# Two attention stages issued in text order, laid out by clocks that the generator keeps

## The chip, the core and the metric

One core of a Trainium2 chip runs the whole program as one launch. The metric is the device time of that launch in microseconds (us). Differences of more than about 0.2% can be told from the runs.

## What is computed

The input is x, 512 tokens by 1024, in float32. It goes through two blocks.

The first block has two layers. Each is a feed-forward part, a mixer and a second feed-forward part, with a conditioning vector that scales, shifts and gates each part. The mixer of the first layer is the stick-breaking attention ("stick" from here), that of the second a linear recurrence. The second block has two "hybrid" layers: three kinds of attention beside each other (A: blocks, B: the 128 best keys by an index score, C: dilated groups), whose outputs are gated, projected and added. The stick mixer and the common part of A, B and C are:

```python
z = q[block] @ k.T                       # q already scaled, 16 heads, 4 query blocks of 128
log_keep = where(s < t, log_sigmoid(-z), 0)
later = reverse_cumsum(log_keep) - log_keep
w = where(s < t, exp(log_sigmoid(z) + later), 0);  o = w @ v
...
p = softmax(where(ok, q @ k.T * hd ** -0.5, -inf));  o = p @ v
merged = sum over branches of sigmoid(m_g[branch]) * (y[branch] @ w_br[branch])
x = x + merged @ w_out
```

## The kernel before

All weights come as one stream of 128x1024 chunks in the order of their use. Each 512 columns are split in two float32r parts, `wh` (ScalarE, ACT here) and `wl` (GpSimd, POOL here, or VectorE, DVE here), and every product is three matmuls of 512 columns: high by high, high by low, low by high. TensorE (PE here) has 13646 matmuls. PSUM has eight banks: four `mm` for the projections, two `z` for scores, one `T` for transposes and one `o` for attention outputs.

A Python generator writes the program. Its projections are plain loops (`proj`, `proj_tok`), which after each three matmuls call `pump`. Everything else is a coroutine: it issues some instructions and then yields a number of us after which its next step is due. The due times count in `vt`, a clock that only the matmuls advance. So between the matmuls of a projection stand the steps of attention that are due by then.

A "pack" is one unit of attention that fills a bank with scores: for heads with a causal mask the query blocks 0 and 2, or 3, or 1 and 1 of two heads; for C two or four blocks. In stick (`unit`, lines 1108 to 1150) a pack is: scores in a `z` bank; two sigmoids on ACT (`keep`, `beta`); on POOL an affine_select for each diagonal block, on DVE a scan for each of the one or two segments (`R`, line 1133) and a product for each (line 1137); four transposes to the `T` bank; a copy on ACT and a difference on DVE for the two parts of the result (`wide`, lines 1026 and 1029). When a head has its four blocks, eight matmuls make its output in the `o` bank (`causal_pv`), and an ACT copy and a DVE sum (`osum`, line 1005) join its parts. In the hybrid layers (`softmax`, lines 1387 to 1422) a pack is, for each segment, the scores and behind them at once the masked maximum on DVE (line 1399), then the exponential with its sum on ACT (line 1411), a reciprocal and a scaling (line 1417), the transposes and the same evacuation.

Between `begin` (whose block is issued as written) and the end of stick, and in both hybrid layers, the order on the engines is not the text's: a scheduler behind the generator puts instructions of all engines in the order that its own estimates give.

Stick ends with the output product in two parts (`STICK_PARTS`): `wo0` for head pairs 0 to 5, `wo1` for pairs 6 and 7, each for eight row blocks m, added to x; after the second, `whole(m)` makes the squares (`sq`) and the parts of the next input (`gH`, `gL`). A hybrid layer ends with the branch products (`br`, each after its gate `mg`) in the order of `HYBRID_ORDER`; at the first of branch 1, `reload` reads x back, and in the first hybrid layer multiplies its eight tiles by two factors on DVE (line 1794). Then come the products of `w_out`, which read `hH` and `hL` (lines 1820 and 1823).

## Time and profile before

| | us |
|---|---|
| median of three runs | 3132.39 (3127.72 to 3134.24) |
| the profiled execution | 3133.14 |
| its span, first to last instruction | 3131.3 |
| PE busy | 3007.2 (96%) |
| DVE, ACT, POOL busy | 1921.7, 1321.7, 1072.8 |
| granted PE clock, mean | 0.986 |

Between the span and the execution's time lie 1.8 us. The stages stand in this order in the span: two feed-forward parts around stick (415 to 700), two around the recurrence, then the hybrid layers (1985 to 2545 and 2545 to 3113) and the last norm. A matmul's busy time overlaps that of the next, so that a busy PE need not be at its peak.

### The profile page before, as it was taken

The numbers are of one execution on the slowest core, as the hardware profiler recorded it, in microseconds if no ns is written. First come the engines' busy times: TensorE is split into PE (matmuls) and PEld (weight loads), VectorE is DVE, ScalarE is ACT, GpSimd is POOL, SyncE is SP. The second block draws the span as 40 slices with busy tenths as digits, with TensorE's granted clock in tenths as the row PEclk, the third lists the DMA queues.
The fourth block names the chain that finished last, engine by engine and source line by source line (L and its number), as shares of the span: only waits on it lengthen the run. The fifth ranks groups of instructions, "written<-read, shape, count | busy, mean of one in ns | idle before, by whom it ended". The sixth has DMA issues, their size and how long they took to land. (4 is left out here: it accounts for less than half of the span.)

```text
span 3131.3 us, 39192 instructions
## 1 busy us (share of the span) xinstructions
PE 3007.2 (96%) x13752; PEld 2474.4 (79%) x13752; DVE 1921.7 (61%) x3455; ACT 1321.7 (42%) x2520; POOL 1072.8 (34%) x828
## 2 busy tenths in 40 slices
PE   7999999989999999999899999999999999999998
PEld 5788877778888888887788888888787778878776
DVE  7844467685445654569773334587766547877643
ACT  3332245543332333226543333355455434655552
POOL 4455744440001100025430002433334674333356
PEclk9999999999999999999999999999999999999999
DMA  6454545324343344542222223543441336324322
GB/s 243 163 195 172 209 120 142 102 68 147 130 140 128 135 162 149 181 175 74 88 88 101 94 105 111 136 135 105 120 132 62 108 124 177 103 88 128 102 78 91
DMA packets 132358, 400.03 MB, mean 128 GB/s; under 512 B 18496, under 2 KB 19008, under 8 KB 132160
## 3 DMA queue, kind: packets, MB, share of 16 engines
q1 hardware_dynamic: 132160, 397.51, 39.1%
q8 instruction: 109, 1.79, 0.2%
q14 instruction: 89, 0.73, 0.1%
HBM read 342.91 MB, written 6.30 MB: 112 GB/s over the span
## 5 line engine op out<-in xcount | busy, mean ns | idle before, releaser
L503 POOL TENSOR_TENSOR wl<-raw,wh 128x512 fp32r<-128x512 f32 x576 | 803.0, 1402 | 940.9 <-ACT wh L497 897.2
L497 ACT CAST wh<-raw 128x512 fp32r<-128x512 f32 x968 | 596.4, 620 | 1152.7 <-PE mm L417 993.0
L417 PE MATMUL mm<-hH,wh 128*128 128x512 f32 x1584 | 620.9, 392 | 12.4 <-ACT ge L1284 9.8
L417 PE MATMUL mm<-hL,wh 128*128 128x512 f32 x1584 | 620.3, 392 | 4.1 <-DVE hL L722 3.4
L417 PE MATMUL mm<-hH,wl 128*128 128x512 f32 x1584 | 619.4, 391 | 0.3 <-POOL wl L503 0.3
L503 DVE TENSOR_TENSOR wl<-raw,wh 128x512 fp32r<-128x512 f32 x394 | 290.0, 737 | 363.0 <-ACT wh L497 360.6
L417 PE MATMUL mm<-gH,wh 128*128 128x512 f32 x1016 | 409.7, 403 | 1.9 <-ACT wh L497 1.8
L417 PE MATMUL mm<-gH,wl 128*128 128x512 f32 x1016 | 401.9, 396 | 1.3 <-POOL wl L503 1.3
L417 PE MATMUL mm<-gL,wh 128*128 128x512 f32 x1016 | 401.6, 395 | 0.0
L417 PEld LDWEIGHTS mm<-hH,wh 128*128 128x128 f32 x1584 | 299.1, 189 | 76.0 <-ACT ge L1284 10.2
L417 PEld LDWEIGHTS mm<-hL,wh 128*128 128x128 f32 x1584 | 299.0, 189 | 68.5 <-DVE hL L722 5.5
L417 PEld LDWEIGHTS mm<-hH,wl 128*128 128x128 f32 x1584 | 298.9, 189 | 62.3 <-POOL wl L503 0.7
L485 DVE CUSTOM_DVE_ANT_0 raw<-raw,cact 128x1024 f32<-128x1024 f32 x144 | 209.2, 1456 | 177.4 <-DMA raw<-ws 167.0
L417 PE MATMUL mm<-aH,wh 128*128 128x512 f32 x704 | 273.9, 389 | 0.0
L417 PE MATMUL mm<-aH,wl 128*128 128x512 f32 x704 | 273.9, 389 | 0.0
L635 POOL TENSOR_TENSOR sq<-x 128x512 f32<-128x512 f32 x7 | 8.1, 1151 | 736.9 <-DVE x L970 710.0
L417 PEld LDWEIGHTS mm<-gH,wl 128*128 128x128 f32 x1016 | 192.4, 189 | 42.1 <-POOL wl L503 2.6
L417 PEld LDWEIGHTS mm<-gH,wh 128*128 128x128 f32 x1016 | 193.4, 190 | 36.2 <-ACT wh L497 2.3
L417 PEld LDWEIGHTS mm<-gL,wh 128*128 128x128 f32 x1016 | 193.3, 190 | 32.9
L1029 DVE TENSOR_TENSOR wide<-T,wide 128x128 fp32r<-128x128 f32 (+3 forms) x192 | 94.2, 511 | 102.5 <-ACT wide L1026 93.8
L417 PEld LDWEIGHTS mm<-aH,wh 128*128 128x128 f32 x704 | 132.1, 188 | 27.6
L417 PEld LDWEIGHTS mm<-aH,wl 128*128 128x128 f32 x704 | 132.1, 188 | 27.4
(302 smaller groups left out, 4825.0 us busy)
## 6 DMA issues: line engine op xcount, KB each, us to landing
raw<-ws SPq DMA_DIRECT2D x629, 512.0 KB, 3.3
ks<-rH SPq DMA_DIRECT2D x80, 128.0 KB, 3.1
kl<-rL SPq DMA_DIRECT2D x80, 128.0 KB, 2.4
qs<-rH SPq DMA_DIRECT2D x56, 128.0 KB, 3.9
qs<-rL SPq DMA_DIRECT2D x56, 128.0 KB, 3.9
keep<-ws SPq DMA_DIRECT2D x16, 256.0 KB, 5.7
ks<-qkH SPq DMA_DIRECT2D x32, 128.0 KB, 2.8
kl<-qkL SPq DMA_DIRECT2D x32, 128.0 KB, 2.4
```

The costliest lines, as they stand in the source:

```text
L417: self.nc.tensor.matmul(out, lhsT, rhs, start=start, stop=stop, skip_group_check=True)
L485: nc.vector.tensor_tensor_reduce(raw, raw, self.cact, 1.0, 0.0, OP.mult, OP.add, accum_out=self.mods[vec][:, m:m + 1])
L497: nc.scalar.copy(h, w)
L503: eng.tensor_tensor(l, w, h.bitcast(F32), OP.subtract)
L635: nc.gpsimd.tensor_tensor(q, self.x[m], self.x[m], OP.mult)
L1029: nc.vector.tensor_tensor(dst(pt[1], o, n, step), src(c, n, step), dst(pt[0], o, n, step).bitcast(F32), OP.subtract)
```

## The change

Stick and both hybrid layers are built inside `planned`, which makes the order on PE, DVE, ACT and POOL that of the text; SP, which issues the DMAs, keeps the scheduler. To write a good text order, the generator now keeps a clock for DVE, ACT and POOL as well: `Front` and `Timed` wrap the engines, and `clocked` gives each instruction a start (when its engine is free and its operands are made), a length by formula, and an end. A matmul moves `vt` to when its operands are made. A bare `yield` means: when the instructions that this step issued have ended. `rel` gives a bank back at that time, and `room` starts a pack only while at most two heads are in work.

In `softmax` all scores of a pack come first and then the maxima. In stick the two segments of a pack are scanned and multiplied in one instruction each, over 512 columns, with one of three masks, and one affine_select does both diagonals: of 64 scans, products and affine_selects 40 are left. The parts `oH` and `oL` of stick's output are made as each pair of heads ends, and its output product is cut in pairs 0 to 3 and 4 to 7. In the hybrid layers five gates of branch 1 move ahead of the products of branch 2, and the factors of the norm are made by a coroutine beside the first projection. PE has the same 13646 matmuls.

```diff
-HYBRID_ORDER += _each(2, "mg") + _each(2, "br") + _each(1, "mg") + _each(1, "br") + [f"out{m}" for m in (0, *range(2, KD))]
+HYBRID_ORDER += (_each(2, "mg") + _each(1, "mg")[:5] + _each(2, "br") + _each(1, "mg")[5:] + _each(1, "br")) + [f"out{m}" for m in (0, *range(2, KD))]
...
-STICK_PARTS = range(0, 6), range(6, 8)
+STICK_PARTS = range(0, 4), range(4, 8)
...
-        "k_stick": np.concatenate([zero, stick], 1),
+
+        "k_stick": np.concatenate([stick, zero[:, :256], stick, zero, stick, zero[:, :128], stick, zero[:, :128], stick], 1),
...
+    @contextlib.contextmanager
+    def planned(self):
+
+        E = mybir.EngineType
+        self.timed = True
+        for e in self.clock:
+            self.clock[e] = max(self.clock[e], self.vt)
+        with self.tc.manual_schedule(engines={E.PE, E.DVE, E.Activation, E.Pool}):
+            yield
+        self.timed = False
+
...
+    def clocked(self, engine, op, args, kw):
+        aps = [x for x in (*args, *kw.values()) if hasattr(x, "tensor")]
+        out, ins = aps[0], aps[1:]
+        if "accum_out" in kw:
+            ins = [x for x in ins if x is not kw["accum_out"]]
+        n = 1
+        for q in max((x.shape[1:] for x in aps), key=lambda d: [int(np.prod(d))]):
+            n *= q
+        bank = any(x.space == bass.MemoryType.PSUM for x in ins)
...
+        start = max([self.clock[engine]] + [self.made.get(x.tensor.name, 0.0) + 0.035 for x in aps])
+        if engine == "vector":
+            d = 0.15 + n / 960.0
+            if op == "reciprocal":
+                d = 0.15 + n * 0.0062
+            elif op == "tensor_tensor_scan":
+                d = 0.15 + n / 480.0
+            elif op in ("stream_shuffle", "match_replace", "tensor_tensor_reduce"):
+                d += 0.07
+            if strided:
+                d += n * 0.0008
+            if not bank and n > 8 and op not in ("max", "match_replace"):
+                for a, b in self.pool_runs:
+                    d += 0.58 * max(0.0, min(b, start + d) - max(a, start))
...
+        end = start + d
+        self.clock[engine] = end - over
+        self.made[out.tensor.name] = end
+        if "accum_out" in kw:
+            self.made[kw["accum_out"].tensor.name] = end
...
+    def matmul_at(self, out, ins, cost, fresh):
+        t = max([self.vt] + [self.made.get(x.tensor.name, 0.0) + 0.054 for x in ins])
+        if fresh:
+            t = max(t, self.read.get(out.tensor.name, 0.0) + 0.054)
+        self.vt = (t if self.timed else self.vt) + cost
+        self.made[out.tensor.name] = self.vt + 0.17
...
+        if d is None:
+
+            d = max(0.05, self.last - self.vt + 0.05)
...
+        if not self.timed or self.op_end <= self.vt:
+            self.live[tag] -= n
+            return
+
+        def later():
+            yield self.op_end - self.vt
+            self.live[tag] -= n
+        self.spawn(later())
...
+    def room(self, heads):
+
+        me = object()
+        self.line.append(me)
+        while self.line[0] is not me or len(self.apart | set(heads)) > 2:
+            yield 0.2
+        self.line.pop(0)
+        self.apart |= set(heads)
 
...
         def unit(pk):
+            yield from self.room([head for head, _ in pk])
...
-            yield 1.5
+            yield
             R = self.t("R")
-            for head, b, c, w in segs:
-                dg = beta[:, c + w - 128:c + w]
+            mask = masks[{0: 0, 3: 1, 1: 2}[pk[0][1]]]
+
+            d = [c + w - 128 for _, _, c, w in segs]
+            dg = beta[:, d[0]:d[0] + 128]
+            if len(d) == 1:
                 nc.gpsimd.affine_select(dg, dg, [[-1, 128]], OP.is_gt, 0.0, base=0, channel_multiplier=1)
-                nc.vector.tensor_tensor_scan(R[:, c:c + w][:, ::-1], keep[:, c:c + w][:, ::-1],
-                                             mask[:, 512 - w:512][:, ::-1], 1.0, op0=OP.mult, op1=OP.max)
-            yield 2.1
-            for head, b, c, w in segs:
-                nc.vector.tensor_tensor(beta[:, c:c + w - 1], beta[:, c:c + w - 1], R[:, c + 1:c + w], OP.mult)
-            yield 1.5
+            else:
+                dg = bass.AP(tensor=dg.tensor, offset=dg.offset, ap=[list(dg.ap[0]), [d[1] - d[0], 2], [1, 128]])
+                nc.gpsimd.affine_select(dg, dg, [[0, 2], [-1, 128]], OP.is_gt, 0.0, base=0, channel_multiplier=1)
+            nc.vector.tensor_tensor_scan(R[:, ::-1], keep[:, ::-1], mask[:, ::-1], 1.0, op0=OP.mult, op1=OP.max)
+            yield
+            nc.vector.tensor_tensor(beta[:, 0:511], beta[:, 0:511], R[:, 1:512], OP.mult)
+            yield
             T = yield from self.get("T")
             for i in range(4):
                 self.transpose(T[:, 128 * i:128 * i + 128], beta[:, 128 * i:128 * i + 128])
             yield from self.causal_evac(T, pk)
-            yield 1.0
+            yield
             for head, b, c, w in segs:
                 self.left[head] -= 1
                 if self.left[head] == 0:
...
+                h = self.t("oH", dt=F32R)
+                nc.scalar.copy(h, out)
+                yield
+                l = self.t("oL", dt=F32R)
+                nc.vector.tensor_tensor(l, out, h.bitcast(F32), OP.subtract)
+                yield
...
+        yield from self.room([head for head, _, _ in pk])
...
-            at = (mx[:, i:i + 1], sm[:, i:i + 1]) if store is None else store(head, b)
-            segs.append((c, w, at))
+            segs.append((c, w, (mx[:, i:i + 1], sm[:, i:i + 1]) if store is None else store(head, b)))
+            c += w
+        for (head, b, _), (c, w, at) in zip(pk, segs):
             nc.vector.tensor_tensor_reduce(T[:, c:c + w], z[:, c:c + w], mask(head, b, w), 1.0, -3.0e38, OP.add, OP.max,
                                            accum_out=at[0])
...
-                    self.stick()
+                    with self.planned():
...
-            self.hybrid(l)
+            with self.planned():
...
```

PE in the first hybrid layer, where the fourth pack of four C blocks is scored; `z` is the bank, `ks`, `kl` and `qs` the keys and queries, `mm` a projection. Before:

```order
L417 MATMUL z_18833<-ks_18647,qs_18641 128x128
L417 MATMUL z_18833<-kl_18653,qs_18641 128x128
L417 MATMUL mm_18777<-gH_15365,wh_18684 128x512
L417 MATMUL mm_18777<-gL_15366,wh_18684 128x512
L417 MATMUL mm_18777<-gH_15365,wl_18685 128x512
L417 MATMUL z_18833<-ks_18647,qs_18641 128x128
L417 MATMUL z_18833<-kl_18653,qs_18641 128x128
L417 MATMUL mm_18778<-gH_15365,wh_18684 128x512
L417 MATMUL mm_18778<-gL_15366,wh_18684 128x512
L417 MATMUL mm_18778<-gH_15365,wl_18685 128x512
```

And now:

```order
L547 MATMUL z_18784<-ks_18640,qs_18634 128x128
L547 MATMUL z_18784<-kl_18646,qs_18634 128x128
L547 MATMUL z_18784<-ks_18640,qs_18634 128x128
L547 MATMUL z_18784<-kl_18646,qs_18634 128x128
L547 MATMUL z_18784<-ks_18640,qs_18634 128x128
L547 MATMUL z_18784<-kl_18646,qs_18634 128x128
L547 MATMUL z_18784<-ks_18640,qs_18634 128x128
L547 MATMUL z_18784<-kl_18646,qs_18634 128x128
L547 MATMUL mm_18677<-gH_15620,wh_18665 128x512
L547 MATMUL mm_18677<-gL_15621,wh_18665 128x512
```

The eight scores of the pack, which stood in pairs with projections between, now stand together, and the projections follow.

DVE at the end of stick; `R` is the scan, `beta` the product, `wide` the part of the transposed weights, `osum` the sum of a head, `oL` the part for the output product, `x` the sum with the output product, `wshift` work for the next stage. Before:

```order
L1029 TENSOR_TENSOR wide_5570<-T_5606,wide_5569 128x128
L1029 TENSOR_TENSOR wide_5570<-T_5606,wide_5569 128x3x128
L1202 SCALAR_TENSOR_TENSOR x_178<-mm_5616,mod_1767,x_178 128x512
L1029 TENSOR_TENSOR wide_5570<-T_5649,wide_5569 128x4x128
L1005 TENSOR_TENSOR osum_5602<-jt_5688,o_5676 64x512
L429 TENSOR_TENSOR oL_5697<-osum_5369,oH_5695 128x512
L1202 SCALAR_TENSOR_TENSOR x_252<-mm_5656,mod_1767,x_252 128x512
L503 TENSOR_TENSOR wl_5700<-raw_5431,wh_5699 128x512
L536 TENSOR_SCALAR wshift_5703<-raw_5431,mod_2475 128x512
L538 SCALAR_TENSOR_TENSOR wshift_5703<-raw_5431,mod_2475,wshift_5703 128x512
L429 TENSOR_TENSOR oL_5711<-osum_5602,oH_5709 128x512
```

And now:

```order
L328 TENSOR_TENSOR wide_5429<-T_5509,wide_5428 128x2x128
L328 TENSOR_TENSOR wide_5515<-T_5509,wide_5514 128x2x128
L328 TENSOR_TENSOR beta_5507<-beta_5507,R_5518 128x511
L328 SCALAR_TENSOR_TENSOR R_5551<-keep_5530,stick_3133 128x512
L328 TENSOR_TENSOR beta_5532<-beta_5532,R_5551 128x511
L328 TENSOR_TENSOR wide_5515<-T_5544,wide_5514 128x128
L328 TENSOR_TENSOR wide_5515<-T_5544,wide_5514 128x3x128
L328 TENSOR_TENSOR osum_5543<-jt_5554,o_5534 64x512
L328 TENSOR_TENSOR wide_5515<-T_5560,wide_5514 128x4x128
L328 TENSOR_TENSOR osum_5543<-jt_5576,o_5567 64x512
L328 TENSOR_TENSOR oL_5581<-osum_5543,oH_5579 128x512
L328 SCALAR_TENSOR_TENSOR x_92<-mm_5485,mod_1767,x_92 128x512
```

The sums of x with the first part of the output product (the last is `x_252`), which stood between the last packs, are now over before them, and the last pack's steps stand by themselves.

DVE in the first hybrid layer, where x is read back; `sig<-mm,inv` is a gate, `sig<-sig,mm` frees the bank of a branch product. Before:

```order
L1800 TENSOR_TENSOR sig_20785<-mm_20745,inv_15868 128x512
L1800 TENSOR_TENSOR sig_20823<-mm_20787,inv_15868 128x512
L1810 SCALAR_TENSOR_TENSOR sig_20451<-sig_20451,mm_20849 128x512
L1794 SCALAR_TENSOR_TENSOR x_20825<-x_20825,vecs,inv_15882 128x512
L1794 SCALAR_TENSOR_TENSOR x_20827<-x_20827,vecs,inv_15882 128x512
L1810 SCALAR_TENSOR_TENSOR sig_20507<-sig_20507,mm_20867 128x512
L1794 SCALAR_TENSOR_TENSOR x_20829<-x_20829,vecs,inv_15882 128x512
L1794 SCALAR_TENSOR_TENSOR x_20831<-x_20831,vecs,inv_15882 128x512
L1794 SCALAR_TENSOR_TENSOR x_20833<-x_20833,vecs,inv_15882 128x512
L1794 SCALAR_TENSOR_TENSOR x_20835<-x_20835,vecs,inv_15882 128x512
L1794 SCALAR_TENSOR_TENSOR x_20837<-x_20837,vecs,inv_15882 128x512
L1810 SCALAR_TENSOR_TENSOR sig_20583<-sig_20583,mm_20883 128x512
```

And now:

```order
L328 TENSOR_TENSOR sig_20684<-mm_20631,inv_15785 128x512
L328 TENSOR_TENSOR sig_20722<-mm_20686,inv_15785 128x512
L328 TENSOR_TENSOR sig_20760<-mm_20724,inv_15785 128x512
L328 SCALAR_TENSOR_TENSOR x_20762<-x_20762,vecs,inv_15803 128x512
L328 SCALAR_TENSOR_TENSOR x_20764<-x_20764,vecs,inv_15803 128x512
L328 SCALAR_TENSOR_TENSOR x_20766<-x_20766,vecs,inv_15803 128x512
L328 SCALAR_TENSOR_TENSOR x_20768<-x_20768,vecs,inv_15803 128x512
L328 SCALAR_TENSOR_TENSOR x_20770<-x_20770,vecs,inv_15803 128x512
L328 SCALAR_TENSOR_TENSOR x_20772<-x_20772,vecs,inv_15803 128x512
L328 SCALAR_TENSOR_TENSOR x_20774<-x_20774,vecs,inv_15803 128x512
L328 SCALAR_TENSOR_TENSOR x_20776<-x_20776,vecs,inv_15803 128x512
L328 SCALAR_TENSOR_TENSOR sig_20242<-sig_20242,mm_20786 128x512
```

The eight scalings of x, which stood between the first branch products, now all stand ahead of them.

## Rows read from the trace of the kernel before

**Rows 1.** Busy time of each engine by stage; columns as in the first row.

```profile
core 0: us, PE busy (x) PEld busy (x) DVE busy (x) ACT busy (x) POOL busy (x), PEclk, DMA share, GB/s
...
415.00:672.00 257.00, 239.87 (x1156) 195.90 (x1155) 182.27 (x288) 140.17 (x280) 115.24 (x125) 0.97 0.40 111
672.00:700.00 28.00, 21.46 (x96) 17.92 (x95) 24.80 (x41) 10.65 (x19) 12.35 (x9) 0.88 0.23 76
...
1985.00:2545.00 560.00, 536.44 (x2583) 441.04 (x2582) 384.10 (x884) 283.02 (x616) 255.54 (x195) 0.99 0.39 113
2545.00:3113.00 568.00, 551.11 (x2644) 453.94 (x2644) 365.92 (x852) 279.86 (x613) 264.34 (x207) 0.99 0.36 110
...
```

**Rows 2.** PE in order of time, two dense matmuls: start, duration.

```profile
1000.18 0.39 PE L417 MATMUL mm<-wide,wh 128*128 128x512 f32 x1
1000.41 0.39 PE L417 MATMUL mm<-aH,wl 128*128 128x512 f32 x1
...
```

**Rows 3.** As rows 1, seven stretches at half clock: the third, the sum.

```profile
682.90:689.70 6.80, 5.12 (x16) 4.47 (x17) 5.72 (x17) 0.62 (x1) 1.28 (x1) 0.50 0.24 77
...
sum 37.60, PE 33.84 PEld 27.72 DVE 28.51 ACT 13.68 POOL 9.48; mean PE 4.83 PEld 3.96 DVE 4.07 ACT 1.95 POOL 1.35
```

**Rows 4.** Waits of PE from 415 to 700: total us, times, longest.

```profile
PE o L417 <- DVE sq L639: 6.5, 1, 6.5
...
PE mm L417 <- DVE oL L429: 0.3, 1, 0.3
```

**Rows 5.** Waits of PE in the first hybrid layer, 1985 to 2545.

```profile
PE z L417 <- DVE mx L1399: 5.0, 5, 2.3
PE T L421 <- ACT T L1417: 3.5, 8, 0.9
...
PE mm L417 <- ACT hH L1820: 1.7, 1, 1.7
...
PE mm L417 <- DVE sig L1810: 1.6, 2, 1.0
...
PE T L421 <- ACT T L1411: 0.5, 1, 0.5
```

**Rows 6.** Waits of PE in the second hybrid layer, 2545 to 3113.

```profile
PE T L421 <- ACT T L1417: 3.5, 8, 1.0
...
PE mm L417 <- DVE hL L1823: 0.2, 1, 0.2
```

**Rows 7.** Groups of stick, 440 to 672: busy us, mean ns | idle before.

```profile
L1124 ACT ACTIVATE keep<-z 128x512 f32<-128x512 f32 x40 | 24.3, 606 | 10.1 <-PE z L417 9.4
...
L1133 DVE TENSOR_TENSOR_SCAN R<-keep,stick 128x512 f32<-128x512 f32 x16 | 20.2, 1263 | 4.4 <-ACT keep L1124 4.4
...
L1137 DVE TENSOR_TENSOR beta<-beta,R 128x511 f32<-128x511 f32 x16 | 13.2, 822 | 0.9
...
L1029 DVE TENSOR_TENSOR wide<-T,wide 128x512 fp32r<-128x512 f32 x16 | 10.9, 683 | 8.3 <-ACT wide L1026 8.2
...
L429 DVE TENSOR_TENSOR oL<-osum,oH 128x512 fp32r<-128x512 f32 x8 | 6.8, 858 | 3.2 <-ACT oH L427 3.1
```

**Rows 8.** Groups of the hybrid layer on ACT and DVE, 1985 to 2545.

```profile
L1411 ACT ACTIVATE T<-T,nm 128x128 f32<-128x128 f32 x48 | 19.2, 400 | 29.9 <-DVE nm L1408 15.0 <-DVE nm L1405 14.4
L1411 ACT ACTIVATION_READ_ACCUMULATOR T<-T,nm 128x1 f32 x96 | 18.0, 187 | 0.0
...
L1399 DVE CUSTOM_DVE_ANT_0 T<-z,hc 128x128 f32<-128x128 f32 x48 | 13.6, 284 | 15.3 <-PE z L417 15.2
```

**Rows 9.** DVE in order of time, where x comes back.

```profile
2482.68 0.69 DVE L1800 TENSOR_TENSOR sig<-mm,inv 128x512 f32<-128x512 f32 x1 [4.68 <-PE mm L417]
...
2485.32 2.45 DVE L1794 SCALAR_TENSOR_TENSOR x<-x,vecs,inv 128x512 f32<-128x512 f32 x2
...
2488.30 6.95 DVE L1794 SCALAR_TENSOR_TENSOR x<-x,vecs,inv 128x512 f32<-128x512 f32 x5
```

**Rows 10.** Waits of DVE in the first hybrid layer, as rows 4.

```profile
DVE wide L1029 <- ACT wide L1026: 42.9, 25, 3.8
```

More of the change, by code (lines that the diff above doesn't have):

```diff
@@ L338, in __init__ @@
         self.lines = {t: [] for t in self.BANKS}
+        self.line, self.apart = [], set()
+    @contextlib.contextmanager
[6 more added lines that the diff above has]
+            yield
+        self.timed = False
+    def clocked(self, engine, op, args, kw):
[7 more added lines that the diff above has]
+        bank = any(x.space == bass.MemoryType.PSUM for x in ins)
+        wide = [x for x in ins if int(np.prod(x.shape[1:])) > 8]
+        strided = any(abs(x.ap[-1][0]) > 1 for x in (out, *wide) if len(x.ap) > 1)
+        start = max([self.clock[engine]] + [self.made.get(x.tensor.name, 0.0) + 0.035 for x in aps])
[12 more added lines that the diff above has]
+                    d += 0.58 * max(0.0, min(b, start + d) - max(a, start))
+            over = 0.082
+        elif engine == "scalar":
+            d = (0.162 if bank else 0.2) + n / 1210.0
+            if isinstance(kw.get("bias"), type(out)) or isinstance(kw.get("scale"), type(out)):
+                d += 0.09
+            if "accum_out" in kw:
+                d += 0.187
+            if strided:
+                d += n * 0.001
+            over = 0.1
+        else:
+            two = len([x for x in ins if int(np.prod(x.shape[1:])) > 8]) > 1
+            d = 0.12 + n / (440.0 if two else 900.0)
+            over = 0.045
+            self.pool_runs = [q for q in self.pool_runs if q[1] > start - 8.0] + [(start, start + d)]
+        end = start + d
+        self.clock[engine] = end - over
+        self.made[out.tensor.name] = end
+        if "accum_out" in kw:
+            self.made[kw["accum_out"].tensor.name] = end
+        for x in ins:
+            self.read[x.tensor.name] = end
+        self.op_end = end
+        self.last = max(self.last, end)
@@ L350, in step @@
     def step(self, g):
+        before, self.last = self.last, 0.0
         try:
@@ L594, in proj_tok @@
             for b in range(4):
-                out, first = banks[b]
+                if kt == 0:
+                    outs.append(banks(b))
+                out, first = outs[b]
                 out = out[:, :used]
@@ L601, in proj_tok, with banks, get @@
                 self.pump()
+    def banks(self, tags, out):
+        def get(b):
+            out.append(self.bank(tags[b]))
+            return out[b], True
+        return get
     def mod_end(self, vec, m, n):
@@ L663, in spread @@
             self.nc.vector.tensor_scalar(d[:, 128 * b:128 * b + 128], self.ident, y[:, b:b + 1], None, OP.mult)
-        ps = self.bank(tag)
-        return d, ps
+        return d
+    def spread(self, y, tag):
+        d = self.diagonal(y)
+        return d, self.bank(tag)
     def spread_mm(self, d, ps):
@@ L1054, in causal_pv @@
                 self.mm(ps[:, 128 * kt:512], v(kt), pt[part][:, 512 * kt:512 * kt + 512 - 128 * kt], kt == 0 and part == 0, True)
+        self.apart.discard(head)
         return ps
@@ L1059, in stick @@
         nc = self.nc
-        mask = self.t("stick")
-        nc.sync.dma_start(mask, self.io["k_stick"])
+        masks = [self.t("stick") for _ in range(3)]
+        for i, t in enumerate(masks):
+            nc.sync.dma_start(t, self.io["k_stick"][:, 512 * i:512 * i + 512])
         V = {}
@@ L1178, in stick @@
             if name[0] == "v":
-                banks = [self.bank("mm") for _ in range(4)]
-                self.proj_tok(name, stat, [(b, True) for b in banks])
+                banks = []
+                self.proj_tok(name, stat, self.banks(["mm"] * 4, banks))
                 self.spawn(v_evac(n, banks))
@@ L1452, in factors @@
         def factors():
+            late = max(self.made.get(q.tensor.name, 0.0) for q in self.sq.values())
+            yield max(0.1, late - self.vt + 0.1)
             st, ys = self.stats(tag="o")
@@ L1462, in factors @@
             self.rel("o")
+            inv["row"] = row
             if self.twice:
-                d, bc = self.spread(ys[0], "o")
-                self.spread_mm(d, bc)
+                bc = yield from self.get("o")
+                self.spread_mm(ds[1], bc)
                 inv["x"] = self.t("inv")
@@ L1479, in idx_evac @@
         def idx_evac(ps):
+            while "row" not in inv:
+                yield 0.2
             kh, kl = yield from self.rope(ps[0])
@@ L1491, in v_evac @@
         def v_evac(ps, tags, heads, key):
+            while "token" not in inv:
+                yield 0.2
             for b in range(4):
@@ L1769, in driver, with attention @@
                     yield 0.5
+        self.spawn(factors(), 1.0)
         ps = self.proj("idx", self.hmov)
-        factors()
         self.spawn(idx_evac(ps))
         tags = ["mm", "z", "z", "T"]
-        banks = [self.bank(t) for t in tags]
-        self.proj_tok("vab", stat, [(b, True) for b in banks])
+        banks = []
+        self.proj_tok("vab", stat, self.banks(tags, banks))
         self.spawn(v_evac(banks, tags, 7, "AB"))
-        self.need(lambda: len(iw) == 4 and "ready" in iq)
-        self.spawn(choose())
-        self.spawn(driver())
+        def attention():
+            while len(iw) < 4 or "ready" not in iq:
+                yield 0.3
+            self.spawn(choose())
+            self.spawn(driver())
+        self.spawn(attention())
         sig = {}
```

171 lines of the change are left out of this document (103 added, 68 removed).

## The prediction

> **What bounds the kernel now.** I read the busy times by stage first [rows 1]. In the four stretches that the change rebuilds PE is busy 239.87 of 257, 21.46 of 28, 536.44 of 560 and 551.11 of 568 us: idle for 17.13, 6.54, 23.56 and 16.89, together 64.1. DVE comes next with 384.1 of 560, ACT and POOL are half idle, the DMA share is 0.4 or less. So PE bounds every one of these stages, and its work is the same 13646 matmuls afterwards: the change can only take away time in which PE stands or runs slowly. How much that is, three views tell.
>
> First the idle time, 64.1.
>
> Second, what the busy time hides. Two dense matmuls start 0.23 us apart and each is shown for 0.39 [rows 2]: a busy PE counts each matmul 0.16 longer than it costs. The tail of the last one ahead of every wait is therefore lost time shown as busy. The lists of waits have 9 lines with 21 waits in and behind stick [rows 4], 13 lines with 30 in the first hybrid layer [rows 5], 12 with 28 in the second [rows 6] (first and last line shown of each): 79 x 0.16 = 12.6.
>
> Third, the clock. In seven stretches of these stages the granted clock is 0.50, the lower of its two levels; PE is busy for 33.84 us in them [rows 3], work that takes half as long at the higher level: 16.9.
>
> Sum of what there is to gain: 64.1 + 12.6 + 16.9 = 93.6 us. The lists also say who keeps PE waiting: the chains of the attention packs (a `z` bank is not free until its maxima are taken, transposes wait for the weights), and at three places no pack but a hand-over: `o <- sq` 6.5 behind stick [rows 4], `mm <- sig` 1.6 and `mm <- hH` 1.7 at the end of a hybrid layer [rows 5].
>
> **The change part by part.**
>
> *The packs' order.* A pack that is scored at once needs other matmuls beside it until its weights are ready. In a hybrid layer a pack of four C blocks takes 4 x (0.284 + 0.082) for maxima and the small step behind each (0.082: my estimate, of the size of a 128x1 instruction, between 0.05 and 0.19 by [rows 8]), then 4 x (0.400 + 0.187) on ACT: 1.46 + 2.35 = 3.8, some 4.4 with two small steps and the hops. In the order, counted in matmuls of 512 columns at 0.227, PE has between the scores and the transposes of such a pack now 0 to 2.7 us of other matmuls before and 5.4 to 5.6 after. For packs of two segments it is 1.6 to 5.8 before (median about 3.4), 3.4 to 11.9 after (median 5.6). In stick a pack takes 0.606 + 1.263 + 0.822 = 2.69 [rows 7], after the scores, with less than before on DVE since one scan stands for two; all packs but the last few have more than 3.4 beside them. So nearly all waits on packs go. I do not take all: the durations in the generator's clocks are formulas, and an engine that is late by one instruction passes it on. My choice is that one eighth of these waits stays; from both sides it could be none, or half, which is a rival below.
>
> *The end of stick.* The last packs have too little left beside them. From scores to transposes 2.69 against about 1.3 us of matmuls in the order: 1.4 waits. From transposes to output, copy and difference, 0.606 + 0.683 = 1.29, nothing beside. From output to output product an ACT copy, `osum`, `oH`, `oL`: 0.606 + 0.68 + 0.606 + 0.858 = 2.75 (the copies priced as `keep`, `osum` as `wide`) [rows 7], nothing beside, since the first part, that covered it so far, is now issued ahead, as the second pair of order listings shows. Together 5.4. PE stands three times within a few us, so I expect one more stretch at the lower clock, of mean size: 4.83 / 2 = 2.4 [rows 3]. Bounds: 0 (if the four pairs of the second part cover it) and 10. I take 7.8, a new cost.
>
> *Behind stick.* `wo1` has now four pairs, 12 matmuls for each m, 2.72 us instead of 1.36. DVE has per m a sum, squares and a difference, three instructions between 0.683 and 0.858 [rows 7], 2.2: it lagged before, which is the 6.5 on `sq`, and keeps pace now. Left is the last m, 2.0. The half-clock stretch that stood there (5.12 busy, 2.6 lost [rows 3]) goes with the wait.
>
> *The return of x.* The eight scalings now all stand ahead of the evacuations of branch 1 on DVE. x lands, by the start of the first, 2485.32 - 2482.68 = 2.64 us after the gate ahead of it; seven of the eight take 2.45 + 6.95 [rows 9], 1.34 each, all eight 10.7; the first evacuation behind them 0.69. PE meanwhile fills its four `mm` banks, 9 matmuls each, 36 x 0.227 = 8.2. So PE waits 2.64 + 10.7 + 0.69 - 8.2 = 5.8, where it waited 1.6 before on `sig` [rows 5]. Bounds: 0, if the load of x, issued from SP, comes early, and 14, if no bank is free when it starts. The next wait, 1.7 on `hH` [rows 5], stays. In the second layer the scalings are absent, and I leave 1.0 for its end.
>
> *Edits at nothing.* The 24 scans, products and affine_selects fewer relieve DVE and POOL, which are busy 182.27 and 115.24 of 257 [rows 1]: hidden behind PE. The two mask loads more on SP stand in the begin of the program; if that cover failed, each would cost about the landing time of x, 2.64. The five gates moved ahead of branch 2 cost PE the same matmuls and DVE the same 0.69 each [rows 9]; they only lengthen the time that five `sig` tiles live. The eager `oH`, `oL` are the same instructions at another place. The factors beside the first projection: few instructions off PE, covered by it.
>
> *The sum.* Left behind: 7.8 + 2.0 + 5.8 + 1.7 + 1.0 = 18.3. Of the 93.6 the places named above made up 6.5 + 2.6 + 1.6 + 1.7 = 12.4; of the other 81.2 one eighth stays, 10.2. 93.6 - 18.3 - 10.2 = 65.1. The profiled execution took 3133.1, so 3068.0 by its own time; the median is 0.7 lower, and I predict 3067, 2.1% faster.
>
> *A rule of the skill that speaks against it.* In [rows 10] DVE has stood 42.9 us, in 25 waits of up to 3.8, at `wide`, whose other half ACT had not yet made; whatever stood behind it waited too, though a scheduler had chosen that order. The Trainium skill, page "TensorE: Matmul & The Clock Gate", section "Architectural detail: the array is 16× 32×32, not 1× 128×128", says that ScalarE and VectorE take their instructions strictly first in, first out, and that TensorE only pulls weight loads ahead. The row agrees with it. By this rule an order fixed by formula turns each late instruction into a delay of all packs behind it; the fourth rival below is what that would make of the time here.
>
> **Rivals.**
> 1. Nearly everything goes: the end of stick is covered by the second part's first pairs, and x comes early. Then 93.6 is gained: 3133.1 - 93.6 - 0.7 = 3039. For it: DVE is free for a third of the time [rows 1]. Against: the chain at the end of stick has nothing beside it in the order.
> 2. Half of the waits come back at other places, because DVE is late by more than the clocks think: of 81.2 half stays, 40.6 instead of 10.2: 3067 + 30 = 3097, and up to 3127 if nearly all do. I put its middle at 3110.
> 3. The change does not do what it says, since the matmuls that are moved between the waits leave others uncovered: within 0.2%, 6.3 us (what a measurement of this kernel can just tell from no change), 3132.
> 4. Slower, by one mechanism: DVE, in the fixed order, stands at a `wide` or a maximum whose operand is late, while a ready instruction of the other head waits behind it; the pack's bank comes free late and PE stands, once per pack. There are 40 packs in stick and 46 in each hybrid layer, 132. All the gain is eaten at 93.6 / 132 = 0.71 us per pack, more than that is slower. The 42.9 / 25 = 1.7 us of a mean wait [rows 10] show that such delays are of that size; at 1 us per pack the loss is 132 and the time 3132 + 132 - 94 = 3170. Against it: PE is not held up by most of those 42.9 us today, and after the change a pack has 2 us more cover.
>
> **How the numbers follow.** My forecast, with its own range 3050 to 3095: 0.62. Rival 1, 3039: 0.12. Rival 2, 3110: 0.16. Rival 3: 0.03. Rival 4: 0.07. The range for 8 in 10 takes in the forecast, most of rival 1 and the near half of rival 2, by the bounds on the end of stick, the return of x and the share that stays: 3038 to 3116. Faster by over 0.2%: 0.62 + 0.12 + nearly all of 0.16, less the part of rival 2 that ends above 3126: 0.88. Within: 0.04. Slower: 0.08.
>
> **What would show it.** Right: PE idle in the hybrid layers falls from 23.6 and 16.9 to under 12 and 6, the lines `z <- mx` and `T <- T` of the waits all but vanish, of seven half-clock stretches at most three are left. A new wait of PE of 4 to 7 us on the evacuation behind the scalings of x, and three waits of 1 to 3 us at the end of stick, on DVE and ACT; no wait of 6.5 on `sq`. Wrong: PE waits spread over all packs, with DVE waiting on ACT's `wide` for more than 42.9 us (rival 4); waits of the same total at other lines (rival 2); no wait at all where x returns, or at stick's end (rival 1). My number fails most easily at the eighth that stays, which no row gives.

## The result, and the profile after

The changed kernel takes 3084.97 us (3082.79 to 3085.68, four runs) against 3133.31 in the same session: a ratio of 0.9847, 95% interval 0.983 to 0.9864. Its profiled span is 3084.0. The median is 18 us above the 3067 forecast and inside the range; 48 us were won where 65 were forecast.

Where they came from is read best between landmarks of PE that both traces have. *Stick* is from the first matmul of the down product ahead of it to the first of the up product in the feed-forward part behind it; *H0* from the first of the down product ahead of the first hybrid layer to the first of that layer's output product; *H1* from there to the same place in the second layer. Stretches in us, of the profiled runs (the experiments' are told below):

| kernel | stick | H0 | H1 | median of the runs |
|---|---|---|---|---|
| before | 421.4 | 648.6 | 567.8 | 3133.3 |
| after | 423.6 | 620.2 | 545.0 | 3085.0 |
| e1 pairs 0-5, 6-7 | 426.5 | 620.6 | 544.0 | 3086.8 |
| e2 stick left to the scheduler | 422.7 | 619.7 | 544.9 | 3083.4 |
| e3 hybrids left to the scheduler | 425.4 | 631.0 | 556.1 | 3110.0 |
| e4 maxima between the scores | 424.4 | 679.3 | 601.6 | 3203.4 |
| e5 before, scores first alone | 418.2 | 633.2 | 556.9 | 3105.7 |
| e6 gL later | 423.1 | 622.0 | 544.8 | 3085.4 |
| e7 gL later, pairs 0-5, 6-7 | 417.9 | 620.2 | 547.6 | 3081.2 |
| e8 keys 8 us | 423.6 | 619.9 | 540.6 | 3082.2 |
| e9 scan twice, pairs 6, 7 | 441.6 | 620.1 | 543.6 | 3103.0 |
| e10 scan twice, pairs 2, 3 | 432.4 | 621.2 | 543.2 | 3094.4 |
| e11 e7 and hybrid keys 8 us | 419.1 | 621.6 | 539.4 | 3075.9 |
| e12 e7 and hybrid keys 10 us | 417.0 | 615.8 | 538.8 | 3067.6 |

Stretches of unchanged code differ by up to 3.2 us between profiles (stick in before and e5). The hybrid layers won 28.4 and 22.8 us; stick won nothing (2.2 us longer).

Busy times by stage, moved to the same landmarks (columns as in [rows 1], whose four stages these answer to):

```profile
417.40:677.40 260.00, 239.33 (x1161) 195.90 (x1160) 182.47 (x243) 139.13 (x279) 116.02 (x100) 0.97 0.39 108
677.40:704.40 27.00, 22.23 (x96) 18.39 (x95) 24.00 (x39) 11.44 (x21) 10.49 (x8) 0.87 0.28 96
...
1990.80:2522.40 531.60, 521.50 (x2580) 441.56 (x2579) 368.88 (x856) 280.50 (x618) 262.84 (x196) 1.00 0.39 119
2522.40:3067.50 545.10, 536.36 (x2643) 454.56 (x2641) 355.57 (x853) 276.74 (x612) 270.40 (x206) 1.00 0.38 115
```

PE is idle for 10.1 and 8.7 us in the hybrid layers (23.6 and 16.9 before), and for 20.7 and 4.8 around stick (17.1 and 6.5). In the third row PE's busy time itself fell by 14.9 us with the same matmuls: the tails ahead of waits and the half-clock stretches are in it, as the prediction had them, and delays too short for the lists, which the prediction left out. They can be counted in the trace from one matmul's start to the next. Steps that were more than 0.02 us over the median step of their form, at the full clock and without a listed wait, were 231 in the first hybrid layer and 226 in the second before, 22.4 and 21.8 us in all; after they are 122 and 117, 10.0 and 9.5 us.

The waits of PE from 417.4 to 704.4, against [rows 4] (the helpers of the changed kernel give nearly all instructions the lines L328, L547 and, for transposes, L551):

```profile
PE o L547 <- DVE sq L328: 4.8, 1, 4.8
PE T L551 <- DVE beta L328: 4.5, 6, 2.3
PE mm L547 <- DVE v L328: 3.5, 3, 1.9
PE z L547 <- DMA kl<-qkL: 3.3, 2, 1.8
PE mm L547 <- DVE qk L328: 2.3, 1, 2.3
PE mm L547 <- ACT oH L328: 2.0, 1, 2.0
PE T L551 <- DVE wide L328: 1.9, 1, 1.9
PE mm L547 <- DVE qkL L328: 1.0, 1, 1.0
PE o L547 <- ACT wide L328: 0.7, 1, 0.7
PE T L551 <- ACT beta L328: 0.5, 1, 0.5
PE z L547 <- DMA ks<-qkH: 0.4, 1, 0.4
PE o L547 <- DVE wide L328: 0.2, 1, 0.2
```

Before, the same stretch had these lines beside the two in [rows 4]:

```profile
PE o L417 <- DVE wide L1029: 3.9, 3, 2.0
PE T L421 <- DVE beta L1137: 3.5, 6, 1.0
PE T L421 <- DVE wide L1029: 3.5, 6, 1.1
PE z L417 <- ACT beta L1126: 3.1, 1, 3.1
PE mm L417 <- DVE qkL L1090: 1.3, 1, 1.3
PE z L417 <- DMA ks<-qkH: 0.9, 1, 0.9
PE mm L417 <- DVE v L1072: 0.4, 1, 0.4
```

And of the first hybrid layer, 1990.8 to 2522.4, against [rows 5]:

```profile
PE mm L547 <- DVE sig L328: 2.0, 1, 2.0
PE z L547 <- DMA kl<-rL: 2.0, 2, 1.5
PE mm L547 <- DVE v L328: 2.0, 1, 2.0
PE T L551 <- ACT T L328: 1.1, 4, 0.5
```

In the hybrid layer the packs' lines are gone or small (`z <- mx` 5.0 to none, `T <- T` 3.5 to 1.1). In stick the waits are as long as before, on other lines. Those on packs (`wide`, `beta`) fell from 14.0 to 7.8, of which 3.9 stand at the end; hand-overs of projections (`v`, `qk`, `qkL`) and loads of keys, which a scheduler had moved out of the way, rose from 2.6 to 10.5.

### The profile page after: what moved, and what is told of

It is laid out like the page before. It is cut to its first block, busy times and chain, and to the rows that moved or that the text cites. A ratio compares the mean times of both kernels' runs of the same rounds, so it can differ in the third digit from the quotient of the medians.

```text
span 3084.0 us, 39072 instructions
## 1 busy us (share of the span) xinstructions
PE 2977.1 (97%) x13752; PEld 2475.4 (80%) x13752; DVE 1902.0 (62%) x3409; ACT 1312.9 (43%) x2520; POOL 1085.0 (35%) x802
## 5 line engine op out<-in xcount | busy, mean ns | idle before, releaser
L328 POOL TENSOR_TENSOR wl<-raw,wh 128x512 fp32r<-128x512 f32 x574 | 815.3, 1427 | 905.1 <-ACT wh L328 852.2
L328 ACT CAST wh<-raw 128x512 fp32r<-128x512 f32 x968 | 596.0, 620 | 1063.3 <-PE mm L547 926.9
L547 PE MATMUL mm<-hH,wh 128*128 128x512 f32 x1584 | 622.1, 393 | 13.6 <-ACT ge L328 9.8
L547 PE MATMUL mm<-hL,wh 128*128 128x512 f32 x1584 | 620.6, 392 | 2.6 <-DVE hL L328 2.6
L547 PE MATMUL mm<-hH,wl 128*128 128x512 f32 x1584 | 619.7, 391 | 0.0
L328 DVE TENSOR_TENSOR wl<-raw,wh 128x512 fp32r<-128x512 f32 x396 | 290.3, 735 | 363.4 <-ACT wh L328 360.7
L547 PE MATMUL mm<-gH,wh 128*128 128x512 f32 x1016 | 407.2, 401 | 6.2 <-DVE v L328 3.9
L547 PE MATMUL mm<-gH,wl 128*128 128x512 f32 x1016 | 398.5, 392 | 1.5 <-POOL wl L328 1.5
L547 PE MATMUL mm<-gL,wh 128*128 128x512 f32 x1016 | 397.8, 392 | 0.0
L547 PEld LDWEIGHTS mm<-hH,wh 128*128 128x128 f32 x1584 | 299.6, 189 | 77.4 <-ACT ge L328 10.2
L547 PEld LDWEIGHTS mm<-hL,wh 128*128 128x128 f32 x1584 | 299.7, 189 | 67.0 <-DVE hL L328 5.3
L547 PEld LDWEIGHTS mm<-hH,wl 128*128 128x128 f32 x1584 | 299.5, 189 | 62.5
L328 DVE CUSTOM_DVE_ANT_0 raw<-raw,cact 128x1024 f32<-128x1024 f32 x144 | 207.8, 1446 | 187.0 <-DMA raw<-ws 180.1
L547 PE MATMUL mm<-aH,wl 128*128 128x512 f32 x704 | 274.0, 389 | 0.0
L547 PE MATMUL mm<-aH,wh 128*128 128x512 f32 x704 | 273.9, 389 | 0.0
L328 POOL TENSOR_TENSOR sq<-x 128x512 f32<-128x512 f32 x7 | 7.6, 1086 | 730.7 <-DVE x L328 730.7
L547 PEld LDWEIGHTS mm<-gH,wl 128*128 128x128 f32 x1016 | 191.4, 188 | 44.7 <-POOL wl L328 2.7
L547 PEld LDWEIGHTS mm<-gH,wh 128*128 128x128 f32 x1016 | 192.1, 189 | 42.0 <-issue 4.3
L547 PEld LDWEIGHTS mm<-gL,wh 128*128 128x128 f32 x1016 | 192.1, 189 | 35.0
L547 PEld LDWEIGHTS mm<-aH,wl 128*128 128x128 f32 x704 | 132.1, 188 | 27.6 <-POOL wl L328 0.4
L547 PEld LDWEIGHTS mm<-aH,wh 128*128 128x128 f32 x704 | 132.1, 188 | 27.5
L547 PE MATMUL mm<-wide,wh 128*128 128x512 f32 x384 | 149.4, 389 | 0.0
```

Source lines behind the costliest of these rows:

```text
L328: r = f(*args, **kw)
L547: self.nc.tensor.matmul(out, lhsT, rhs, start=start, stop=stop, skip_group_check=True)
```

## The experiments

**e3 and e5: what the fixed order gives, and what scores-first gives.** e3 leaves the hybrid layers of the changed kernel to the scheduler; e5 puts one edit into the kernel before.

```diff
-            with self.planned():
-                self.hybrid(l)
+            self.hybrid(l)
```

> The changed kernel, but both hybrid layers are left to the scheduler, with the scores of a pack first as in the changed kernel. The changed kernel won 28.4 and 22.9 us in these layers. Theory A: the fixed order carries it, because only the generator leaves 5 us of projections between the scores of a pack and its transposes; then the gain is lost: about 3130 (3120 to 3140). Rival B: the scores standing first carry it, and the scheduler does as well with them: 3090 or under. Between, say 3105 to 3115, if each carries half.

```diff
             segs.append((c, w, at))
+            c += w
+        for (head, b, _), (c, w, at) in zip(pk, segs):
             nc.vector.tensor_tensor_reduce(T[:, c:c + w], z[:, c:c + w], mask(head, b, w), 1.0, -3.0e38, OP.add, OP.max,
                                            accum_out=at[0])
-            c += w
```

> The kernel before with one part of the change alone: in the hybrid layers all scores of a pack first and then its maxima; the scheduler keeps the order of everything. Left to the scheduler, the changed kernel's hybrid layers (which have scores first) took 631.0 and 556.1 us against 648.6 and 567.8 before and 620.2 and 545.0 in the fixed order. Theory A: those 17.6 and 11.7 are what scores-first gives, alone: 3133 - 29 = 3104 (3098 to 3110). Rival B: they come from the other edits (five gates moved, room for two heads, factors beside the first projection), and scores-first gives under 8: over 3122.

e3: 3110.0, half lost, as neither theory alone had it. e5: 3105.7 against 3131.4 (0.9916, 0.9901 to 0.9931), theory A. The two agree stretch by stretch (631.0 and 633.2, 556.1 and 556.9), no further apart than unchanged code, so under the scheduler the moved gates, `room` and the factors are not seen to be worth anything. Scores-first gives 15.4 and 10.9 us; the step from e3 to the changed kernel, the fixed order, 10.8 and 11.1. Each takes away its own kind of wait. In the kernel before, scores waited for maxima (both hybrid layers together):

```profile
PE z L417 <- DVE mx L1399: 7.7, 9, 2.3
PE z L417 <- DVE stat L1399: 3.3, 6, 0.8
```

In e5 and in e3 these lines are gone. What is left there is led by transposes that wait for their weights, 8.8 us in e5, and in e3:

```profile
PE T L551 <- ACT T L328: 13.3, 23, 1.5
```

The fixed order brings that line to 2.0 in the changed kernel.

**e4: what the fixed order is without it.**

```diff
-            c += w
-        for (head, b, _), (c, w, at) in zip(pk, segs):
+            at = segs[-1][2]
             nc.vector.tensor_tensor_reduce(T[:, c:c + w], z[:, c:c + w], mask(head, b, w), 1.0, -3.0e38, OP.add, OP.max,
                                            accum_out=at[0])
+            c += w
```

> The changed kernel with the maxima of a pack written again between its scores, nothing else undone; the order on each engine is then the same, only the text order between scores and maxima differs. Theory A: a score waits for the maximum of the segment before it, since both are in one bank (the kernel before shows scores waiting for maxima, 5.0 and 2.7 us in the two layers, though it put projections between); with a fixed order nothing is put between, and some 100 segments that are not the first of their pack each wait 0.4 to 0.7 us: 40 to 70 us slower, 3125 to 3155. Rival B: the two don't meet, since they touch other columns of the bank, and scores-first does nothing by itself in a fixed order: 3085 within 3.

3203.4: 118 us slower than the changed kernel, 2.4% slower than before (1.0237, 1.022 to 1.0254). The waits of PE in its hybrid layers:

```profile
PE z L547 <- DVE stat L328: 28.3, 64, 1.1
PE z L547 <- DVE mx L328: 27.1, 36, 3.1
```

100 scores wait for the maximum ahead of them, 55.4 us idle: theory A in kind, though it had 3125 to 3155. The rest of the 118 was not taken apart: other waits grew too (loads of keys from 5.6 to 9.9, `mm <- v` from 3.9 to 6.2), and the mean granted clock is 0.978 for 0.987. The scores of a pack stand together on PE in both; only what a score waits for differs, and the steps around them that the generator's clocks shift with it (the order is not word for word the same, as the expectation had it). So the two edits are not a sum: the fixed order loses without scores-first and wins with it.

**e1 and e2: stick's cut, and stick's order.**

```diff
-STICK_PARTS = range(0, 4), range(4, 8)
+STICK_PARTS = range(0, 6), range(6, 8)
```

> The changed kernel with one thing undone: stick's output product again in pairs 0 to 5 and 6 to 7. The changed kernel's stick, from its begin to the next feed-forward, takes 303.7 us where the old one took 301.7, although I had forecast 24 less. Theory A: the end of stick (waits of 1.2 to 2.4 us on beta, wide, wide, oH between 641 and 654, and matmuls at half clock behind them, 9.7 us in all) is what the cut into halves costs; with the old cut the first part stands between the last packs again and covers them. The wait on sq behind it grows from 4.9 to about 6.7. Then stick gets 6 to 8 us shorter: 3078. Rival B: what the packs wait for only moves, since the last chain is as long as before: the same time within 2 us, 3085.

```diff
-                    with self.planned():
-                        self.stick()
+                    self.stick()
```

> The changed kernel, but stick is left to the scheduler; the merged scans, the halves and the hybrid layers' fixed order stay. Theory A: the fixed order takes nothing from stick's waits and adds none (about 37 us of lost PE time in both kernels), so the stage stays at 302 to 306 us and the run at 3085 to 3088. Rival B: the fixed order does shorten the packs' waits, and the halves and the loads of the stacked keys eat that; then without it stick is 10 us or more longer: 3095 or over. Rival C: the fixed order itself makes stick's new waits (on v, qk and qkL, where the next projection stands behind an evacuation that the order put late, 9 us together); then stick gets shorter by about that: 3076.

e1: 3086.8, rival B. Of the changed kernel's lines at stick's end, `T <- beta` 1.1, `T <- wide` 1.9 and `mm <- oH` 2.0, the old cut leaves none, but PE now waits for DVE there (640 to 692):

```profile
PE mm L547 <- DVE x L328: 7.2, 4, 2.9
PE o L547 <- DVE sq L328: 3.7, 1, 3.7
PE mm L547 <- DVE oL L328: 1.5, 1, 1.5
```

e2: 3083.4, stick 0.9 shorter: by the time theory A, the fixed order is worth nothing in stick. By the lines it is not idle there, but trades one kind of wait for another. Left to the scheduler, stick has 0.2 us of waits on hand-overs and keys where the fixed order has 10.5, but these on packs (417 to 706), where the fixed order has 7.8 on all lines:

```profile
PE T L551 <- DVE wide L328: 12.1, 11, 2.4
PE T L551 <- DVE beta L328: 5.3, 7, 2.0
```

**e6 and e7: DVE behind stick.** In the changed kernel DVE stands 1.31 us at the first five of the eight `gL`; two of them (start, us, [idle before <- what ended it]):

```profile
665.55 1.34 DVE L328 SCALAR_TENSOR_TENSOR gL<-x,mod,gH 128x512 fp32r<-128x512 f32 x1 [1.31 <-ACT gH L328]
666.81 0.74 DVE L328 SCALAR_TENSOR_TENSOR x<-mm,mod,x 128x512 f32<-128x512 f32 x1
668.86 1.33 DVE L328 SCALAR_TENSOR_TENSOR gL<-x,mod,gH 128x512 fp32r<-128x512 f32 x1 [1.31 <-ACT gH L328]
```

e6 makes `gL` (`low` in the cut), and two of the sums of squares, one block later; e7 is e6 with the edit of e1.

```diff
-        self.square(m)
...
-        nc.scalar.activation(h, self.x[m], AF.Identity, scale=g)
-        nc.vector.scalar_tensor_tensor(l, self.x[m], g, h.bitcast(F32), OP.mult, OP.subtract)
...
+            for f in self.owed:
+                f()
+            self.owed = []
+            if m < KD - 1:
+                nc.scalar.activation(h, x, AF.Identity, scale=g)
+                self.square(m)
+                self.owed.append(low)
...
```

> The changed kernel; in the two planned stages the parts of the next input are made one row block later: ACT makes gH before the square, and DVE's gL of block m (and its sum of squares) stands behind the sum of x of block m+1, not ahead of it. In the changed kernel DVE stands 1.31 us at each gL behind stick, waiting for ACT, with the next sum of x behind it: 3.35 us per block where PE brings one each 2.72, so PE waits 4.9 on sq in the end, and 1.2 behind the first hybrid layer. Theory A: it is this standing that makes DVE late; then DVE keeps up and the wait on sq falls to 0 to 1.5: 4 to 6 us less, 3080. Rival B: DVE is late because of its work (weights' parts and shifts at 1.7 us beside POOL) and the wait stays at 4 or more: 3084.

> As the last, and stick's output product again in pairs 0 to 5 and 6 to 7. With that cut alone the waits of the attention's end fell from 9.7 to 2.5 us, but PE then brought a block every 1.36 us, and waits on DVE's sums of x and on sq came to 11.8, so that nothing was won. Theory A: with gL late those fall to about 4 to 6, since DVE needs about 2 us per block: 3085 - 6 to 8 = 3077 to 3079. Rival B: DVE's work per block is itself the bound and the sum of both stays: 3083 to 3087.

e6: 3085.4, the wait on `sq` 3.1 for 4.8, the time the same: more rival B than A, since the standing went and DVE's work beside POOL (shifts and sums of squares of up to 1.75 us that take 0.7 alone) stayed. e7: 3081.2, stick 417.9, between the two theories; the wait on `sq` is 4.8 again, those on `x` fell from 7.2 to 0.7. The stick stretches of e7, e11 and e12 (417.9, 419.1, 417.0) all lie below those of after, e6 and e1 (423.6, 423.1, 426.5): together the two edits give 4.5 to 6.6 us, either alone none.

**e9 and e10: is it DVE's work?** The same ten scans more, at two places; the cut is that of e9, and in e10 the condition is `4 <= pk[0][0] < 8`:

```diff
-            nc.vector.tensor_tensor_scan(R[:, ::-1], keep[:, ::-1], mask[:, ::-1], 1.0, op0=OP.mult, op1=OP.max)
+            for _ in range(2 if pk[0][0] >= 12 else 1):
+                nc.vector.tensor_tensor_scan(R[:, ::-1], keep[:, ::-1], mask[:, ::-1], 1.0, op0=OP.mult, op1=OP.max)
```

> The changed kernel with DVE work added: the scans of stick's last ten packs (pairs 6 and 7) run twice, with the same result; the generator's clocks count both. In the changed kernel DVE is busy 35.9 of the 40 us from 605 to 645, in which these packs run, and whatever I did to the end of stick only moved PE's waits to another line. Theory A: from the last keys to the next stage DVE's work sets the time, so ten more scans of 1.21 us, 12.1, come out nearly whole: stick 10 to 13 us longer, 3095 to 3098. Rival B: PE's own order and the chain of the last pack set it; then only the last two or three packs' scans are seen: 2 to 4 us, 3087 to 3089.

> The same ten scans more, but in pairs 2 and 3, in the middle of stick, where DVE is busy for about 0.7 of the time. Theory A (DVE binds only from about 605 us on): 0 to 4 us, 3085 to 3089. Rival B (DVE binds all of stick, or each pack's chain is seen by PE): 10 us or more, 3095 and over.

e9: 3103.0, stick 18.0 us longer for 12.1 us of scans (ten of 1.21). Theory A in kind and more in size: with DVE behind, PE stands longer and its clock falls. The stretch 605 to 645 in the changed kernel, then in e9 with the one behind it (columns as in [rows 1]):

```profile
605.00:645.00 40.00, 37.86 (x195) 31.38 (x196) 35.92 (x47) 24.02 (x49) 19.66 (x17) 1.00 0.41 112
```

```profile
605.00:625.00 20.00, 17.86 (x88) 14.94 (x89) 16.57 (x19) 10.83 (x21) 11.68 (x9) 1.00 0.65 175
625.00:645.00 20.00, 15.13 (x77) 12.32 (x76) 18.94 (x26) 7.48 (x16) 7.04 (x6) 0.96 0.17 55
645.00:665.00 20.00, 11.71 (x43) 9.83 (x41) 12.63 (x16) 6.86 (x15) 2.31 (x3) 0.61 0.00 0
```

DVE has 0.83 and 0.95 of the first two stretches, while PE's share falls; in the third no engine is full. e10: 3094.4, stick 8.8 us longer, near rival B: in the middle, where DVE had 55.74 of 80 us, 0.7 of what is added to it comes out too. A second scan adds to DVE's work and also lengthens each pack's chain from scores to transposes, and these two runs don't tell the two apart. One or the other, or both, can be felt at either place, at the end most.

**e8, e11, e12: the loads of keys.**

```diff
             ks = self.stack_k(kh, kl)
-            yield 6.0
+            yield 8.0
```

e8 does this in stick (the cut) and in the hybrid layers; e11 in the hybrid layers alone, on top of e7; e12 is e11 with 10.0.

> The changed kernel, but the packs of a pair of heads wait 8.0 instead of 6.0 us of the generator's clock after their stacked keys are sent, in stick and in the hybrid layers. In the changed kernel PE waits for loads of kl and ks at 4.2 us in all in stick and 6 in the two hybrid layers, which the kernel before hardly did (1.05 in stick), because a fixed order cannot go past a key that lands late. Theory A: the price is this wait alone: 6 to 10 us less, 3076. Rival B: the packs that come 2 us later uncover something else, as every move in stick did so far: 3083 to 3088.

> What helped, together: gL one block later and pairs 0 to 5 and 6 to 7 (3081 together, stick 5.7 us shorter than in the changed kernel), and the 8.0 us behind the stacked keys in the hybrid layers alone, where it took the waits on the loads of kl from 4.5 us to 0.3 and 4.7 us off the two layers; in stick it gave nothing. If the two add up: 3085 - 5 - 4 = 3076 (3073 to 3079). If the keys' gain was chance: 3081.

> As the last with 10.0 us behind the stacked keys. At 8.0 hardly a wait on a key is left (0.3 us), so 2 us more can only uncover: same as the last to 5 us slower. If instead the packs' early start is itself a burden (PE then has less projection left for the later packs), it goes on falling: 3 us or more under the last.

e8: 3082.2 (0.9841, 0.9826 to 0.9855), not told apart from the changed kernel by the runs. By its trace rival B holds in stick (423.6 still: the waits on keys, 3.7, are gone, those on `beta` rose from 4.5 to 8.2 and `oL` came with 2.2), theory A in H1 (4.4 less). e11: 3075.9 (0.9821, 0.9808 to 0.9834), the sum that was expected. e12: 3067.6 (0.9798, 0.9784 to 0.9811), 8.3 below e11 where I expected the same or worse; the other reading that I had written, that an early pack is itself a burden, fits. In its hybrid layers PE is idle for 6.7 and 4.5 us (columns as in [rows 1]):

```profile
1983.00:2510.20 527.20, 520.51 (x2580) 441.67 (x2579) 372.79 (x855) 279.52 (x618) 260.72 (x197) 1.00 0.40 121
2510.20:3049.20 539.00, 534.54 (x2643) 453.67 (x2641) 361.18 (x854) 275.02 (x612) 266.28 (x205) 1.00 0.38 115
```

How it works was not taken apart: the lines `z <- DMA` are gone, and so is `mm <- v`, 2.0 in each layer; 12 us and more were not tried. e12 beats both kernels.

## Why the prediction was right, and where it was not

*That PE bounds the stages, and that the order can only give back its waits:* right for the hybrid layers. By the prediction's own terms they held 56.5 of the 93.6 us (40.5 idle, 58 x 0.16 of tails, 6.8 of the clock's 16.9, which lay in their stretches) and were to give 41.4. The packs' waits went, by the mechanism forecast (more projections between scores and transposes). Still the same terms hold 24.3 now: 18.8 idle, 25 waits x 0.16 = 4.0, and 1.5 of the one half-clock stretch left. So they gave 32.2. The layers gave 51.2 because the short delays that no view of before lists, and that the sum had left out, fell by more than half. That they beat their forecast is luck, and so is part of the total: by its own terms the whole change gave 30.6 of the 65.1.

*"So nearly all waits on packs go", one eighth stays:* this step failed in stick, and is the reason for the 18 us. By the sum's terms stick and its tail held 37.1 and were to give 23.8; they hold 38.7 now (25.4 idle, 20 waits x 0.16, 10.1 of the clock), and the stretch is 2.2 longer. That is 26.0 short, of which the 9.8 that the hybrid layers gave over their forecast make good a part. The packs' own waits fell, but seven eighths of all waits could only go if none came in their place, and the sum had no term for what the fixed order adds: the hand-overs of projections and the loads of keys, 10.5 us for 2.6. e2 shows the trade from the other side.

What stands behind it is clearest at the end of stick. DVE was busy from 605 to 645 for 35.19 of 40 us before and is for 35.92 now; the prediction read DVE from the whole stage, 182.27 of 257 [rows 1], and so took the waits there for a question of order. e9 shows what more of its work costs there, and e1 and e6 that moving it alone gives nothing. But 14.2 of the 25.1 us of listed waits lie ahead of 606, where DVE is busy for 0.57 to 0.76 of the time. e10 and e8 show that something holds this part too, since what is added comes out and what is taken away comes back on another line. Whether it is DVE's work or the chain of each pack stays open.

The merged scans, which the prediction expected to relieve DVE and POOL, did not: scans and products took 95.7 us of DVE before and take 88.9, and in all DVE is busy for 182.47 us where it was for 182.27, POOL for 116.02 where it was for 115.24.

*The end of stick, 7.8:* right. The waits are 1.1 + 1.9 + 0.7 + 0.2 + 2.0 = 5.9 (5.4 forecast), and one half-clock stretch stands there, from 650.75 to 657.58, with PE busy for 4.79 us of it, 2.4 lost as forecast. Its part behind the last wait:

```profile
654.10:657.40 3.30, 3.30 (x7) 2.37 (x8) 1.43 (x2) 0.53 (x1) 0.00 (x0) 0.50 0.00 0
```

But the halves alone are not what it costs: without them (e1) as much is lost at `x` and `sq`, and only with `gL` late as well (e7) is something won.

*Behind stick, 2.0 left:* 4.8. The three DVE instructions were sized at 2.2 per block; from one `gL` to the next it took 3.3 to 5.1 for the first seven, of which 1.31 was standing at most of them, and parts of the next stage's weights stood between. Here the rule on strict order, which the prediction cites from the Trainium skill (page "TensorE: Matmul & The Clock Gate", section "Architectural detail: the array is 16× 32×32, not 1× 128×128"), is seen on one line: DVE stood at `gL`, and its next sum of x waited behind it. As a delay of all packs (the fourth rival) it is not seen. DVE's waits at `wide` in the first hybrid layer, 42.9 us in [rows 10], are now

```profile
DVE wide L328 <- ACT wide L328: 8.4, 6, 3.0
```

*The return of x, 5.8:* the wait is there, at the line forecast, and measures 2.0. x landed 1.67 after the gate instead of 2.64, and the eight scalings took 7.1, where the prediction had 10.7 (and the trace of before 10.1):

```profile
2461.70 1.44 DVE L328 SCALAR_TENSOR_TENSOR x<-x,vecs,inv 128x512 f32<-128x512 f32 x2 [0.98 <-DMA x<-xd]
2463.78 5.67 DVE L328 SCALAR_TENSOR_TENSOR x<-x,vecs,inv 128x512 f32<-128x512 f32 x6 [0.64 <-DMA x<-xd]
```

*Of the signs named:* idle 10.1 (under 12) came, 8.7 (under 6) did not; `z <- mx` vanished and the waits at the end of stick came; the 6.5 on `sq` became 4.8 instead of none; of the seven half-clock stretches (37.6 us) five are left (27.3), not three. *Rivals:* the second, waits that come back at other places, is what happened in stick alone; its reason, a DVE later than the clocks think, is not shown. The fourth needed a maximum or a `wide` that holds up all packs; the nearest thing to it is e4, which the change avoids by its one edit in `softmax`.

## What to carry to other kernels

An engine's share over a stage hides the stretch in which it is full: before a wait is put down to order, read the busy time of the engine that PE waits for in that stretch, and double one of its instructions there to see whether the time follows (it tells that the work or the chain through it binds, not which). A stage that takes as long as before can hide two changes that cancel: compare the waits kind by kind. Sum the steps from one matmul's start to the next as well as the listed waits, since some 19 of the 51.2 us that the hybrid layers won were in delays too short for a list. A fixed order is only as good as the dependences that are left in it: take apart first what waits by layout (scores and maxima in one bank), since a scheduler could hide it and text order can't. And when each of two edits gives nothing, the same limit may stand behind both places: try them together.

## What was not expected of the hardware

Some of DVE's work is slower beside POOL. The same scaling of 128x512 took 1.34 us in the kernel before, where POOL was busy for 7.95 of 9.30 us, and 0.72 (the first two) to 0.95 (the next six) in the changed one, where POOL was busy for 2.49 of 7.00. Instructions of 0.74 us at stick's end (`wshift`) take 1.75 beside POOL. It isn't so for those that read a PSUM bank: of the sums `x<-mm,mod,x` of the changed kernel the nine that lay wholly beside a POOL instruction took 0.72 to 0.74. The generator's clocks have a term for this (the loop over `pool_runs` in `clocked`, left out when an operand is in a bank); the sums of the prediction took each duration as its row had it. A duration from the trace is one for the company that it had there.
